# A third PSUM bank in the rotation of two projections, and an earlier load of the first recurrence tile, in a one-layer hybrid backbone

## The chip, the cores and the metric

The kernel runs on one core of a Trainium2 chip. The metric is the device time of one execution in microseconds (us); lower is better. Times of before and after are medians of several runs. One execution was also taken by the hardware profiler; the rows below come from that one.

## What is computed

One layer: a token mixer with three parallel branches, then an expert-choice mixture of experts, for 1024 latent tokens of width 1024 and a prefix of 256 context tokens that only feeds initial states. Cut to what matters here:

```python
proj = h @ p['w_in']                       # h: 1280 x 1024 (context + latents), w_in: 1024 x 7200
u_s5, z, xbc, dt_raw, x_lru, g_lru, gates = split(proj)
ya = s5_branch(u_s5)                       # grouped complex scan, two directions
yb = rmsnorm((ssd_scan(conv(xbc), dt) + D * x) * silu(z)) @ m2_w_out     # Mamba-2, chunks of 128
yc = (rglru_scan(conv(x_lru)) * gelu(g_lru)) @ lru_w_out                 # diagonal recurrence, two directions
g = sigmoid(gates).reshape(.., 3, 1024)
merged = (g[0]*ya + g[1]*yb + g[2]*yc) @ w_o
# then: residual, norm, router, top-k per expert, 16 SwiGLU experts, residual, final norm
```

All large matrix products are made of three passes over operands split into a high and a low part (fp32r), summed in PSUM.

## The kernel before

The program runs through stages whose instructions overlap at the seams. First the modulation and norm of the inputs, which leaves `h` transposed in SBUF as high and low parts (`hxh`, `hxl`). Stage one (pool `p1`) makes the projections `u`, `xbc`, `x_lru` (`xl`) and `g_lru` (`gl`), and the S5 branch, eight groups `hb` one after another (`s5_tab`, `s5_dat`). Stage two (pool `p2`) does the Mamba-2 scan and the RG-LRU recurrence: `states()` carries the chunk states over nine steps, then 32 calls `chunk(g, c)` make the outputs; the four recurrence tiles `lru_tile(t)` are a generator of which the loop takes a step at a time; the projections `z` (8 tasks) and the gates (24 tasks) run in between and fill TensorE. Stage three merges the branches, stage four makes the output product and the routing, stage five the experts.

A projection task loads 128 columns of `w_in` (`load_w`, L117 to L127), splits them on ScalarE and VectorE, and calls `proj_chunk` (L267) for each piece of 512 tokens: 24 matmuls into one PSUM bank (`mm3`, L263 to L265) and an evacuation by ScalarE: `gt` (gelu, L626) for `gl`, `zt` (tanh, L770, with a VectorE step L771 that reads the bank too) for `z`, `gz` (tanh, L778) for the gates. The bank comes from `pbank` (L86), a rotation over two of the eight banks. Five banks belong to a second rotation, `bank`; the last bank has the tag `pm` and is used, in the stretch in question, only by `cx` of `s5_dat` (L526), the context part of the S5 scan.

`lru_tile(t)` begins with a load of the rows `xcd[t]` into `lxc` (L850), a clearing of `lw` on GpSimd (L852), four small loads of weights into `lw` (L855), and casts of both on ScalarE (L858, L863). For t = 0 the program text puts this behind `chunk(0, 0)`.

The order of instructions within each engine is not the text's: outside of the stages whose order is written by hand (stage four on TensorE, stage five), a planner simulates the program when it is built and puts every engine's instructions, SyncE's DMA issues among them, in the order in which its own clock finds them ready; text order is the priority, and evacuations and weight loads are lifted by `high_priority(offset=WPRI)`. On the chip each engine then goes through its queue strictly in that order. A tile of a rotating buffer can be written only when the readers of the tile before it in text order are done.

Of the kernel before, what the change touches and what calls it, by code (L numbers as in the profile page):

```python
# [8 lines left out]
F32 = mybir.dt.float32  # L9
# [9 lines left out]
P = 128  # L19
# [38 lines left out]
def dap(t, off, dims):  # L58
    return bass.AP(tensor=t.tensor, offset=t.offset + off, ap=[list(d) for d in dims])
# [3 lines left out]
def backbone(ctx: ExitStack, tc: tile.TileContext, I, out, dbg=None, stop=None):  # L63
    nc = tc.nc
    V, A, G, T, Y = nc.vector, nc.scalar, nc.gpsimd, nc.tensor, nc.sync
# [14 lines left out]
    psp = psstack.enter_context(tc.tile_pool(name="psp", bufs=1, space=PSUM, reuse_waits="tile"))  # L80
    bankh = [lambda nm: psp.tile([P, 512], F32, tag="b", name=nm, bufs=5)]

    def bank(name):
        return bankh[0](name)

    def pbank(name):  # L86
        return psp.tile([P, 512], F32, tag="pp", name=name, bufs=2)
# [64 lines left out]
    with tc.high_priority(offset=20000):  # L152
        with tc.tile_pool(name="p0", bufs=1, reuse_waits="tile") as p0:
# [26 lines left out]
            pm = bank("pm")  # L180
# [80 lines left out]
    def mm3(ps, wh, wl, xh, xl, nk, first=True, last=True):  # L261
        for k in range(nk):
            T.matmul(ps, wh(k), xh(k), start=(first and k == 0), stop=False)  # L263
            T.matmul(ps, wh(k), xl(k), start=False, stop=False)  # L264
            T.matmul(ps, wl(k), xh(k), start=False, stop=(last and k == nk - 1))  # L265

    def proj_chunk(w, m, nm, evac, c):  # L267
        t0, n, xh, xl, s0 = ((0, 512, hxh, hxl, 0), (512, 512, hxh, hxl, 512), (1024, 256, hch, hcl, 0))[c]
        ps = pbank(f"pj_{nm}_{t0}")
        mm3(ps[:m, :n], lambda k: w[0][:, k, :], lambda k: w[1][:, k, :], lambda k: xh[k][:, s0:s0 + n], lambda k: xl[k][:, s0:s0 + n], KC)  # L270
        with tc.high_priority(offset=WPRI):
            evac(ps, t0, n)
# [7 lines left out]
    xcd = [dr.tile([P, 1283], F32, name=f"xcd{t}") for t in range(4)]  # L280
# [6 lines left out]
    with tc.tile_pool(name="p1", bufs=1, reuse_waits="tile") as p1:  # L287
# [65 lines left out]
        if True:  # L353
# [15 lines left out]
            lr, li = lam[:, 0], lam[:, 1]  # L369
# [311 lines left out]
    with tc.tile_pool(name="p2", bufs=1, reuse_waits="tile") as p2:  # L681
# [7 lines left out]
        la = p2.tile(n3, F32, name="la")  # L689
# [49 lines left out]
        def states():  # L739
            Sp = None  # L740
            v16 = lambda t: t.rearrange("p (h e) -> p h e", h=16)
            for k in range(9):
                st = [bank(f"st{k}_{q}") for q in range(2)]
                for d, c in ((0, cf(k)), (1, cb(k))):
                    xk = p2.tile([P, 1283], F32, tag="xk", name=f"xk{k}{d}", bufs=3)
                    Y.dma_start(xk[:, 0:D].rearrange("p (g e) -> p g e", g=4), xed[c][:, :, 0:256])
                    Y.dma_start(xk[:, D:D + 256], btd[c])
                    xd = p2.tile([P, D], F32, tag="xd", name=f"xd{k}{d}", bufs=2)
                    G.tensor_mul(v16(xd), v16(xk[:, 0:D]), dtd[:, c, d, :, None].to_broadcast([P, 16, 64]))
                    for g in range(4):  # L750
                        T.matmul(st[g // 2][64 * d:64 * d + 64, (g % 2) * 256:(g % 2 + 1) * 256],
                                 xk[:, D + 64 * g:D + 64 * g + 64], xd[:, 256 * g:256 * g + 256], start=True, stop=True)
                Sn = p2.tile([P, D], F32, tag="Sn", name=f"Sn{k}", bufs=2)
                if k > 0:
                    V.tensor_mul(v16(Sn), v16(Sp), decS[:, k, :, None].to_broadcast([P, 16, 64]))
                for q in range(2):
                    sl = slice(q * 512, (q + 1) * 512)
                    if k == 0:
                        V.tensor_copy(Sn[:, sl], st[q])
                    else:  # L760
                        V.tensor_add(Sn[:, sl], Sn[:, sl], st[q])
                if k > 0:
                    Y.dma_start(xed[cf(k + 1)][0:64, :, 256:512], Sn[0:64].rearrange("p (g e) -> p g e", g=4))
                    Y.dma_start(xed[cb(k + 1)][64:128, :, 256:512], Sn[64:128].rearrange("p (g e) -> p g e", g=4))
                Sp = Sn
# [18 lines left out]
        def chunk(g, c):  # L784
# [30 lines left out]
            if c % 4 == 3:  # L815
# [13 lines left out]
                        G.tensor_add(ssum[:, cs], ssum[:, cs], zq[:, t])  # L829
                Y.dma_start(m2_dram[g][:, :, cs], xq)  # L830

        states()
        z_task(0)
        z_task(1)
# [10 lines left out]
        SQE = math.sqrt(EPS)  # L845

        def lru_tile(t):
            lt = lambda nm: p2.tile([P, 1283], F32, tag="xk" if nm in ("lr", "li", "la") else nm, name=f"{nm}{t}", bufs=3 if nm in ("lr", "li", "la") else 1)
            xc = lt("lxc")
            Y.dma_start(xc, xcd[t])  # L850
            lw = p2.tile([P, 2, 2, P], F32, tag="lw", name=f"lw{t}", bufs=1)
            G.memset(lw, 0.0)  # L852
            for e, nm in enumerate(("lru_w_a", "lru_w_x")):
                for hh in range(2):
                    Y.dma_start(lw[64 * hh:64 * hh + 64, e, :, 64 * hh:64 * hh + 64],  # L855
                                dap(I[nm], (2 * t + hh) * 4096, [[64, 64], [8 * 4096, 2], [1, 64]]))
            lwh, lwl = (p2.tile([P, 2, 2, P], F32R, tag=g, name=f"{g}{t}", bufs=1) for g in ("lwh", "lwl"))
            A.copy(lwh, lw)  # L858
            G.tensor_sub(lwl, lw, lwh.bitcast(F32))
            xh_, xl_ = (p2.tile([P, S], F32R, tag="Sn", name=f"lx{g}{t}", bufs=2) for g in "hl")  # L860
            xe_ = p2.tile([P, 2, SC], F32R, tag="lxe", name=f"lxe{t}", bufs=1)
            for o, n, h_, l_ in ((0, S, xh_, xl_), (1027, SC, xe_[:, 0], xe_[:, 1])):
                A.copy(h_, xc[:, o:o + n])  # L863
                G.tensor_sub(l_, xc[:, o:o + n], h_.bitcast(F32))
            yield
            hs = None
            for d in range(2):
                dt_ = 4 * d + t
                col = lambda q: lsc[:, q, dt_:dt_ + 1]
                r, ig = lt("lr"), lt("li")  # L870
                G.memset(r[:, 1024:1027], 0.0)
                G.memset(ig[:, 1024:1027], 0.0)
                for e, dst in enumerate((r, ig)):
                    for (t0, n, h_, l_) in ((0, 512, xh_[:, 0:512], xl_[:, 0:512]), (512, 512, xh_[:, 512:S], xl_[:, 512:S]), (1027, SC, xe_[:, 0], xe_[:, 1])):
                        ps = bank(f"lps{t}{d}{e}{t0}")
                        for q, (w_, x_) in enumerate(((lwh, h_), (lwh, l_), (lwl, h_))):
                            T.matmul(ps[:, :n], w_[:, e, d, :], x_, start=(q == 0), stop=(q == 2))
                        A.activation(dst[:, t0:t0 + n], ps[:, :n], AF.Tanh, bias=lbh[:, e, dt_:dt_ + 1], scale=0.5)
                    yield
                a, q = lt("la"), lt("lq")  # L880
                A.activation(a, r, AF.Exp, scale=col(0), bias=col(0))
                A.activation(q, r, AF.Exp, scale=col(2), bias=col(2))
                A.activation(r, r, AF.Tanh, scale=col(1), bias=col(1))
                V.scalar_tensor_tensor(q, q, 1.0, r, op0=ALU.add, op1=ALU.mult)
                A.activation(q, q, AF.Sqrt)
                V.scalar_tensor_tensor(ig, ig, 1.0, xc, op0=ALU.add, op1=ALU.mult)
                V.scalar_tensor_tensor(ig, q, SQE, ig, op0=ALU.max, op1=ALU.mult)
                if d == 0:
                    V.tensor_tensor_scan(q[:, 1027:1283], a[:, 1027:1283], ig[:, 1027:1283], 0.0, op0=ALU.mult, op1=ALU.add)
                    hs = p2.tile([P, S], F32, tag="xd", name=f"lh{t}", bufs=2)  # L890
                    V.tensor_tensor_scan(hs, a[:, 0:S], ig[:, 0:S], q[:, 1282:1283], op0=ALU.mult, op1=ALU.add)
                else:
                    V.tensor_tensor_scan(q[:, 1027:1283][:, ::-1], a[:, 1027:1283][:, ::-1], ig[:, 1027:1283][:, ::-1], 0.0, op0=ALU.mult, op1=ALU.add)
                    V.tensor_tensor_scan(q[:, 0:S][:, ::-1], a[:, 0:S][:, ::-1], ig[:, 0:S][:, ::-1], q[:, 1027:1028], op0=ALU.mult, op1=ALU.add)
                    V.tensor_add(hs, hs, q[:, 0:S])
                    gl = a[:, 0:S]
                    Y.dma_start(gl, gld[t])
                    V.scalar_tensor_tensor(hs, hs, 0.5, gl, op0=ALU.mult, op1=ALU.mult)
                    Y.dma_start(lru_dram[t], hs)
                yield  # L900
# [46 lines left out]
    with tc.tile_pool(name="p3b", bufs=1, reuse_waits="tile") as p3b:  # L947
# [112 lines left out]
        for d in range(KC):  # L1060
# [5 lines left out]
            for h in range(2):  # L1066
                sl = slice(h * 512, (h + 1) * 512)
                ps = bank(f"bom{d}{h}")
# [42 lines left out]
    li = [dt[0:16, q * P:(q + 1) * P] for q in range(2)]  # L1111
# [230 lines left out]
    with tc.tile_pool(name="p5", bufs=1, reuse_waits="tile") as p5:  # L1342
# [107 lines left out]
        with tc.manual_schedule(engines={mybir.EngineType.DVE, mybir.EngineType.Activation, mybir.EngineType.PE}):  # L1450
# [6 lines left out]
            for s_, (nm, e, j) in enumerate(slots):  # L1457
# [6 lines left out]
                if j == 0:  # L1464
                    tag = {"w1": "h1", "w3": "h3", "w2": "py" if e < 15 else "h1"}[nm]
                    ps = [psp5.tile([P, 512], F32, tag=tag, name=f"{tag}_{nm}{e}{n}", bufs=2) for n in range(2)]
# [125 lines left out]
```

## Time and profile before

| | |
|---|---|
| median of 3 runs | 2032.36 us (2030.41 to 2035.47) |
| profiled execution | 2033.83 us, span of its instructions 2032.0 us |
| TensorE busy | 1878.6 us (92% of the span) |
| VectorE busy | 1583.6 us (78%) |
| ScalarE busy | 1019.4 us (50%) |
| GpSimd busy | 501.1 us (25%) |
| mean granted TensorE clock | 0.965 of full speed |

Rows of an engine's timeline read: start in us, duration in us, engine, line, operation, output<-inputs, shapes, count; in brackets the idle time of that engine just before, and what released it. PE is TensorE, DVE VectorE, ACT ScalarE, POOL GpSimd, SPq the queue of SyncE that issues DMAs. A granted clock of 1.00 is 2.4 GHz, of 0.50 is 1.2 GHz.

### The profile page before, as it was taken

The numbers are of one execution on the slowest core, as the hardware profiler recorded it, in microseconds if no ns is written. First come the engines' busy times: TensorE is split into PE (matmuls) and PEld (weight loads), VectorE is DVE, ScalarE is ACT, GpSimd is POOL, SyncE is SP. The second block draws the span as 40 slices with busy tenths as digits, with TensorE's granted clock in tenths as the row PEclk, the third lists the DMA queues.
The fourth block names the chain that finished last, engine by engine and source line by source line (L and its number), as shares of the span: only waits on it lengthen the run. The fifth ranks groups of instructions, "written<-read, shape, count | busy, mean of one in ns | idle before, by whom it ended". The sixth has DMA issues, their size and how long they took to land.

```text
span 2032.0 us, 26879 instructions
## 1 busy us (share of the span) xinstructions
PE 1878.6 (92%) x9514; PEld 1507.1 (74%) x9514; DVE 1583.6 (78%) x2183; ACT 1019.4 (50%) x1313; POOL 501.1 (25%) x456
## 2 busy tenths in 40 slices
PE   6989999998899999999999999995599999999997
PEld 3678788886666777777777778784488888888885
DVE  4796778876364778887447965599799999999998
ACT  4434444432321765667322122322488887878885
POOL 1463333330053244342000000236201101010142
PEclk8999999998999999999999999998799999999999
DMA  9234334422477676666568863655699999999974
GB/s 326 40 90 116 107 101 117 126 85 69 152 249 215 194 226 187 203 210 198 176 207 298 281 207 125 239 191 201 225 350 405 389 401 393 394 399 394 371 285 166
DMA packets 273127, 462.64 MB, mean 228 GB/s; under 512 B 39968, under 2 KB 167632, under 8 KB 271968
## 3 DMA queue, kind: packets, MB, share of 16 engines
q1 hardware_dynamic: 268672, 445.19, 62.9%
q0 software_dynamic: 4320, 15.73, 3.0%
q8 instruction: 75, 1.23, 0.2%
q14 instruction: 60, 0.49, 0.1%
HBM read 384.44 MB, written 78.51 MB: 228 GB/s over the span
## 4 chain that ended last, share of the span: by engine, by line
PE 36%; DVE 7%; DMA 5%; issue 1%; POOL 1%; SPq 1%; ACT 0%; DVEq 0%; POOLq 0%; ACTq 0%
PE h_w L1472 6%; PE h_w L1473 6%; PE h_w L1474 6%; DMA wm<-in_w_mod_dram 3%; PE py_w L1472 3%; PE py_w L1474 3%; PE py_w L1473 3%; PE wo L1289 2%; PE bom L264 1%; PE bom L263 1%; PE bom L265 1%; DVE tu L1124 1%; PE tb_x L1383 1%; DVE tv L1121 1%; PE tb_h L1383 1%
## 5 line engine op out<-in xcount | busy, mean ns | idle before, releaser
L1367 DVE TENSOR_TENSOR el_w<-er_w,eh_w 128x1024 fp32r<-128x1024 f32 x384 | 459.9, 1220 | 24.7 <-ACT eh_w L1366 11.9
L1366 ACT CAST eh_w<-er_w 128x1024 fp32r<-128x1024 f32 x384 | 403.7, 1052 | 105.7 <-PE h_w L1473 64.7
L1472 PE MATMUL h_w<-eh_w,thi_x 128*128 128x512 f32 x512 | 203.3, 397 | 0.0
L1473 PE MATMUL h_w<-eh_w,tlo_x 128*128 128x512 f32 x512 | 200.5, 392 | 0.0
L1474 PE MATMUL h_w<-el_w,thi_x 128*128 128x512 f32 x512 | 200.2, 391 | 0.0
L263 PE MATMUL pj_gt<-hxh,whi_gt 128*128 128x512 f32 x384 | 153.7, 400 | 8.5 <-ACT gz L778 8.5
L264 PE MATMUL pj_gt<-hxl,whi_gt 128*128 128x512 f32 x384 | 152.9, 398 | 0.0
L265 PE MATMUL pj_gt<-hxh,wlo_gt 128*128 128x512 f32 x384 | 152.2, 396 | 0.0
L1474 PEld LDWEIGHTS h_w<-el_w,thi_x 128*128 128x128 f32 x512 | 96.5, 189 | 20.8 <-DVE el_w L1367 0.2
L1473 PEld LDWEIGHTS h_w<-eh_w,tlo_x 128*128 128x128 f32 x512 | 96.6, 189 | 19.5 <-DVE tlo_x L1391 0.4
L1472 PEld LDWEIGHTS h_w<-eh_w,thi_x 128*128 128x128 f32 x512 | 96.6, 189 | 19.5 <-ACT thi_x L1390 0.2
L1375 POOL DMA_INDIRECT xs<-h2d,idx x16 | 24.0, 1498 | 293.9 <-PE tb_x L1383 273.4
L1472 PE MATMUL py_w<-eh_w,thi_h 128*128 128x512 f32 x240 | 96.4, 402 | 0.0
L1473 PE MATMUL py_w<-eh_w,tlo_h 128*128 128x512 f32 x240 | 93.9, 391 | 0.0
L1474 PE MATMUL py_w<-el_w,thi_h 128*128 128x512 f32 x240 | 93.9, 391 | 0.0
L263 PEld LDWEIGHTS pj_gt<-hxh,whi_gt 128*128 128x128 f32 x384 | 73.3, 191 | 27.3 <-ACT gz L778 10.8
L804 POOL TENSOR_TENSOR dec<-dec,bc 128x512 f32<-128x512 f32 x32 | 64.8, 2024 | 93.2 <-ACT dec L795 86.0
L1408 POOL DMA_INDIRECT accd<-ysm,idx x14 | 49.8, 3560 | 149.3 <-DVE ysm L1406 138.9
L265 PEld LDWEIGHTS pj_gt<-hxh,wlo_gt 128*128 128x128 f32 x384 | 73.2, 191 | 15.9 <-issue 0.2
L264 PEld LDWEIGHTS pj_gt<-hxl,whi_gt 128*128 128x128 f32 x384 | 73.2, 191 | 15.9 <-issue 0.3
L1197 POOL TENSOR_TENSOR r_wo<-r_wo,bc_m 128x1024 f32<-128x1024 f32 x4 | 10.2, 2540 | 279.1 <-DMA mgm<-mgd 138.8
L799 DVE TENSOR_TENSOR rowb<-rowb,XL 128x1024 f32<-128x1024 f32 x32 | 49.9, 1560 | 36.9 <-ACT dec L795 36.9
(649 smaller groups left out, 5046.5 us busy)
## 6 DMA issues: line engine op xcount, KB each, us to landing
er_w<-in_moe_w_dram SPq DMA_DIRECT2D x384, 512.0 KB
rowb<-rowsd SPq DMA_DIRECT2D x32, 512.0 KB
wm<-in_w_mod_dram SPq DMA_DIRECT2D x32, 512.0 KB
raw_gt<-in_w_in_dram SPq DMA_DIRECT2D x24, 512.0 KB
gtd<-gz SPq DMA_DIRECT2D x48, 256.0 KB
xk<-xed SPq DMA_DIRECT2D x18, 512.0 KB
wm<-in_w_mod_dram SPq DMA_DIRECT2D x8, 1024.0 KB
xe<-xed SPq DMA_DIRECT2D x32, 256.0 KB
```

The lines of the kernel that those rows point to most:

```text
L263: T.matmul(ps, wh(k), xh(k), start=(first and k == 0), stop=False)
L264: T.matmul(ps, wh(k), xl(k), start=False, stop=False)
L265: T.matmul(ps, wl(k), xh(k), start=False, stop=(last and k == nk - 1))
L799: V.tensor_sub(rowb, rowb, XL[:, c, :, 4 * g:4 * g + 4][:, :, :, None].to_broadcast(sh))
L804: G.tensor_mul(dec, dec, Cd[:, None, :].to_broadcast([P, 4, P]))
L1289: T.matmul(st4[i]["ps"][n], ms[i][a][:, k], wo[k][b][:, sl], start=(k == 0 and q == 0), stop=(k == KC - 1 and q == 2))
L1366: A.copy(a, raw)
L1367: V.tensor_sub(b, raw, a.bitcast(F32))
L1408: G.indirect_dma_start(out=accd[:, :], out_offset=bass.IndirectOffsetOnAxis(ap=idx[:, e:e + 1], axis=0), in_=yss[e], in_offset=None, compu ...
L1472: T.matmul(ps[n], xa[:, j, :], a[:, sl], start=(j == 0), stop=False)
L1473: T.matmul(ps[n], xb[:, j, :], a[:, sl], start=False, stop=False)
L1474: T.matmul(ps[n], xa[:, j, :], b[:, sl], start=False, stop=(j == KC - 1))
```

## The change

`proj_chunk` counts its calls; each third call takes its bank from the tag `pm` where the task's name begins with z or g, which are `z`, the gates (`gt`) and `gl`. The first part of `lru_tile(t)` (the load of `lxc`, the clearing of `lw`, its four loads) becomes a function `lru_in(t)`; for t = 0 it is called in front of `states()`, for the other tiles where it stood.

```diff
+    pn = [0]
+
     def proj_chunk(w, m, nm, evac, c):
         t0, n, xh, xl, s0 = ((0, 512, hxh, hxl, 0), (512, 512, hxh, hxl, 512), (1024, 256, hch, hcl, 0))[c]
-        ps = pbank(f"pj_{nm}_{t0}")
+        pn[0] += 1
+        ps = psp.tile([P, 512], F32, tag="pm", name=f"pj_{nm}_{t0}", bufs=1) if pn[0] % 3 == 2 and nm[0] in "zg" else pbank(f"pj_{nm}_{t0}")
...
+        lt_ = lambda nm, t: p2.tile([P, 1283], F32, tag="xk" if nm in ("lr", "li", "la") else nm, name=f"{nm}{t}", bufs=3 if nm in ("lr", "li", "la") else 1)
+
+        def lru_in(t):
+            xc = lt_("lxc", t)
+            Y.dma_start(xc, xcd[t])
+            lw = p2.tile([P, 2, 2, P], F32, tag="lw", name=f"lw{t}", bufs=1)
+            G.memset(lw, 0.0)
+            for e, nm in enumerate(("lru_w_a", "lru_w_x")):
+                for hh in range(2):
+                    Y.dma_start(lw[64 * hh:64 * hh + 64, e, :, 64 * hh:64 * hh + 64],
+                                dap(I[nm], (2 * t + hh) * 4096, [[64, 64], [8 * 4096, 2], [1, 64]]))
+            return xc, lw
+
+        lin0 = [lru_in(0)]
         states()
...
         def lru_tile(t):
-            lt = lambda nm: ...
-            xc = lt("lxc")
-            Y.dma_start(xc, xcd[t])
...
+            lt = lambda nm: lt_(nm, t)
+            xc, lw = lin0.pop() if lin0 else lru_in(t)
```

## Rows read from the trace of the kernel before

**Rows 1.** Busy time of stage two and of one stall: stretch, length, engines, granted clock, DMA, GB/s.

```profile
560.00:700.00 140.00, 140.00 (x654) 100.47 (x654) 83.96 (x81) 43.46 (x57) 54.30 (x30) 1.00 0.69 213
700.00:985.00 285.00, 263.79 (x1414) 205.25 (x1413) 232.51 (x194) 183.40 (x236) 102.60 (x63) 0.96 0.64 204
985.00:1043.00 58.00, 55.54 (x246) 45.21 (x246) 18.18 (x17) 22.83 (x22) 1.66 (x1) 1.00 0.53 165
...
720.00:735.00 15.00, 11.69 (x52) 9.26 (x51) 14.97 (x11) 5.00 (x7) 9.60 (x6) 0.78 0.64 210
```

**Rows 2.** Who TensorE waited for, 463 to 560: us in total, times, longest.

```profile
PE pj_z L263 <- DVE zt L771: 6.3, 1, 6.3
PE yp L575 <- DVE ea L568: 5.2, 2, 3.6
PE yp L576 <- DVE eb L571: 3.4, 2, 2.0
PE pj_gl L263 <- ACT gt L626: 2.4, 2, 1.2
```

**Rows 3.** Timeline of all engines around the stall of `z`, at 550.

```profile
549.97 0.40 ACT L863 CAST lxe<-lxc 128x256 fp32r<-128x256 f32 x1 [11.94 <-DMA lxc<-xcd]
...
551.52 0.59 ACT L770 ACTIVATE zt<-pj_z 128x512 f32<-128x512 f32 x1
...
552.15 0.69 DVE L771 SCALAR_TENSOR_TENSOR zt<-zt,pj_z 128x512 f32<-128x512 f32 x1 [12.56 <-ACT zt L770]
...
552.89 0.80 PE L263 MATMUL pj_z<-hxh,whi_z 128*128 128x512 f32 x1 [6.35 <-DVE zt L771]
```

**Rows 4.** SyncE's queue ahead of it: issues of the states' and the tile's loads.

```profile
529.28 6.08 SPq L746 DMA_DIRECT2D xk<-xed  x1
...
542.78 0.32 SPq L850 DMA_DIRECT2D lxc<-xcd  x1
543.20 2.14 SPq L855 DMA_DIRECT2D lw<-in_lru_w_a_dram  x2
```

**Rows 5.** GpSimd's timeline: the states' first multiplication.

```profile
560.60 1.91 POOL L749 TENSOR_TENSOR xd<-xk,dtd 128x1024 f32<-128x1024 f32 x1 [7.05 <-PE prw L726]
```

**Rows 6.** Busy time around the stalls, columns as in Rows 1.

```profile
473.00:478.00 5.00, 4.63 (x20) 4.34 (x20) 2.36 (x10) 0.24 (x1) 0.00 (x0) 0.50 0.01 2
478.00:483.00 5.00, 4.10 (x10) 3.30 (x11) 2.02 (x3) 1.33 (x3) 0.00 (x0) 0.53 0.51 184
507.00:512.00 5.00, 3.82 (x21) 3.63 (x21) 0.00 (x0) 1.17 (x3) 0.53 (x1) 0.70 0.38 105
512.00:523.00 11.00, 11.00 (x49) 9.11 (x50) 0.00 (x0) 1.00 (x2) 0.00 (x0) 1.00 0.35 121
...
553.00:558.00 5.00, 5.00 (x12) 3.92 (x13) 4.36 (x19) 3.86 (x8) 0.53 (x1) 0.52 0.69 216
```

**Rows 7.** TensorE's timeline, 463 to 480: `cx`, the waits of `yp` and of `gl`.

```profile
463.33 1.87 PE L529 MATMUL cx<-U,Pm 128*128 128x32 f32 x16
...
478.90 0.80 PE L263 MATMUL pj_gl<-hxh,whi_gl 128*128 128x512 f32 x1 [1.18 <-ACT gt L626]
```

**Rows 8.** ScalarE's and VectorE's timelines there: evacuations of `gl`, and a weight split.

```profile
478.25 1.08 ACT L626 ACTIVATE gt<-pj_gl 128x512 f32<-128x512 f32 x2
...
492.77 1.23 DVE L126 TENSOR_TENSOR wlo_gl<-raw_gl,whi_gl 128x1024 fp32r<-128x1024 f32 x1 [10.22 <-ACT whi_gl L125]
```

**Rows 9.** Who TensorE waited for, 560 to 1045, the three largest.

```profile
PE pj_gt L263 <- ACT gz L778: 8.5, 6, 3.2
PE yps L813 <- DVE rowb L803: 7.5, 3, 3.6
PE yps L813 <- ACT gz L778: 4.5, 2, 3.3
```

**Rows 10.** VectorE's timeline at the seam to stage three.

```profile
1031.24 1.23 DVE L978 TENSOR_TENSOR ylo_l<-yr_l,yhi_l 128x1024 fp32r<-128x1024 f32 x1 [2.39 <-ACT yhi_l L977]
1042.79 1.76 DVE L958 TENSOR_TENSOR wlo_f<-raw_s,whi_s 128x1536 fp32r<-128x1536 f32 x1 [10.32 <-PE pj_gt L264]
```

More of the change, by code (lines that the diff above doesn't have):

```diff
@@ L847, in lru_tile @@
         def lru_tile(t):
-            lt = lambda nm: p2.tile([P, 1283], F32, tag="xk" if nm in ("lr", "li", "la") else nm, name=f"{nm}{t}", bufs=3 if nm in ("lr", "li", "la") else 1)
-            xc = lt("lxc")
-            Y.dma_start(xc, xcd[t])
[L851 to L856, printed above, removed]
+            lt = lambda nm: lt_(nm, t)
+            xc, lw = lin0.pop() if lin0 else lru_in(t)
             lwh, lwl = (p2.tile([P, 2, 2, P], F32R, tag=g, name=f"{g}{t}", bufs=1) for g in ("lwh", "lwl"))
```

## The prediction

> **What bounds the kernel now.** I read the page's totals first, then the busy time of stage two by stretch, then the waits of TensorE, and last the timelines around each wait. TensorE is busy for 92% of the span, so the question is only where it idles and whether the change reaches those places. Both edits act between the end of stage one (from 463 us) and the last gate (1043 us). In [rows 1] the reader is to see that from 560 to 700 TensorE does not pause at all, that from 700 to 985 it lacks 285.0 - 263.8 = 21.2 us, and that up to 1043 it lacks 2.5 us. In all of that time projections wait to be made, so a microsecond of TensorE that is not idled away is a microsecond off the end of the stage, as long as nothing else is later there. [Rows 10] say how far that holds: the last operand that stage three needs, `ylo_l`, is done at 1031.24 + 1.23 = 1032.5, and the first weights of that stage wait 10.32 us for the last gate. So the loop's tail has some 10 us of room for the gates to end earlier by themselves; where the whole loop moves forward, its tail moves along and more passes through. What follows (merge, output product, experts) starts from there and is moved as a whole.
>
> **The stall of z, and the load that causes it.** [Rows 3] are one chain, read from the bottom: TensorE stands for 6.35 us at a piece of `z` until VectorE's `zt` frees the bank; `zt` waits for ScalarE's `zt`; ScalarE has that in its queue behind the cast `lxe<-lxc`, for which it stood for 11.94 us, until the rows of the recurrence tile landed. Nobody needs that cast soon; it only stands first in a queue that is kept in order. [Rows 4] show why it is late: the load is issued at 542.78, behind the states' loads, and lands at 549.97, 7.2 us later.
>
> The change takes it in front of the states' loads. What it moves there: one clearing on GpSimd, the load of `lxc` (0.32 us of SyncE's time) and four loads of `lw`, two pairs of at most 2.14 us, 4.6 us of SyncE's queue in all [rows 4]. Nine steps of `states` with their loads are passed by it and so come up to 4.6 us later. Cover: the first multiplication of the states waits at 560.60 for something that comes through TensorE (`prw`), not for its rows [rows 5], and TensorE has `z` to do meanwhile. If that cover went, the 4.6 us would fall into the stretch that is busy for 140 of 140 us [rows 1], where they cost nothing until `z` runs out.
>
> Does the load then come in time? ScalarE asked for it at 549.97 - 11.94 = 538.0. In the worst case it inherits the slow issue of 6.08 us in [rows 4], goes out at 535.4 and lands 7.2 us later, at 542.6: `zt` on ScalarE would then start some 1.5 us later (as it did after 549.97), at 544.2, and VectorE's part, 0.6 us after that start and 0.7 us long, would be done at 545.5, before TensorE asks at 552.89 - 6.35 = 546.5. So the 6.35 us go, by this edit alone. Next late there is nothing up to 700 that the rows show.
>
> The third bank reaches the same stall by itself: of three banks in turn, the piece that stalled gets the one that was freed a piece earlier. So these two edits share this term and it is counted once.
>
> The clock comes on top. After the stall twelve matmuls take 5.00 us at a granted clock of 0.52, about the lower level of 1.2 GHz; in an undisturbed stretch 49 take 11.00 us, 0.224 us each, at 1.00 (2.4 GHz) [rows 6]. What the slow stretch loses is its busy time times the missing clock: 5.00 x 0.48 = 2.4 us. **Term one: 6.35 + 2.4 = 8.7 us**, bounds 0 (another instruction of ScalarE's queue takes the cast's place) and 8.7.
>
> **The end of stage one.** `gl` begins with g and takes part in the rotation. [Rows 2] list what TensorE waits for between 463 and 560: 5.2 + 3.4 us for the S5 scan's results (`yp`), 2.4 us for evacuations of `gl`, 11.0 in all beside `z`. Twice the same thing happens: both banks hold finished pieces of `gl`, their evacuation stands behind S5's own output on ScalarE (478.25, [rows 8]), and TensorE has nothing to do while VectorE scans. The first time costs 3.6 + (3.4 - 2.0) + 1.2 = 6.2 us of waiting and, by [rows 6], 4.63 x 0.50 + 4.10 x 0.47 = 4.2 us of clock; the second time 1.6 + 2.0 + 1.2 = 4.8 and 3.82 x 0.30 = 1.1. A third bank lets one more piece run in there: 24 matmuls, 24 x 0.224 = 5.4 us, about as long as the hole. A second effect goes the same way: VectorE idles 10.22 us for a weight split whose buffer the late `gl` holds [rows 8], and the S5 chain of the last group stands behind it.
>
> The added wait: the bank `pm` is also that of `cx`, the S5 context product. The second piece of the first `gl` task now sits between two `cx`, so the last `cx` (16 matmuls, at 463.33, [rows 7]) must wait for that piece's evacuation; at the old place in ScalarE's queue that ends at 478.25 + 1.08 = 479.3. Behind the last `cx` on TensorE is whatever the planner puts there; on VectorE its sums come just ahead of a part that idled for 10.22 us. So it is cheap if `cx` is put behind `yp`, and costs a wait of up to 479.3 - 463.3 = 16 us if something needed stands behind it. Bounds of the term: 11.0 + 5.3 = 16.3 us gained, and, for the added wait less what is gained, nothing gained. **Term two: 7.0 us**, two thirds of the first hole's 10.4, as the row nearest to it is one piece of 5.4 us and a part of the clock; the second hole is left as it is.
>
> One rule speaks against this. The Trainium skill, page "TensorE: Matmul & The Clock Gate", section "HAM oscillation — how this bites in real kernels", reports of a measured kernel that adding double-buffering of PSUM gave no further gain. By it the sum would hold term one alone. The trace agrees only where TensorE is fed without a break, in the 140 us of [rows 1]; in [rows 2, 9] it waits for evacuations by name.
>
> **The gates.** In the loop, waits whose last releaser is the gates' evacuation come to 8.5 us at the gates themselves and 4.5 at `yps` behind them, eight in all, the longest 3.2 and 3.3 [rows 9]. A third bank covers 5.4 us, more than any of them. But the planner knows of the third bank as well, and will run gates further ahead, until it is full again; and the long stalls stand where VectorE is busy for 14.97 of 15 us [rows 1], so that the hole would only reopen at `yps`. Bounds: 13.0 us and the clock of two long stalls (11.69 x 0.22 = 2.6 each) gained, 18.2; or as much lost as the third rival says. **Term three: 2.0 us**, a third of the short ones (8.5 + 4.5 - 3.2 - 3.3 = 6.5).
>
> **Sum.** 8.7 + 7.0 + 2.0 = 17.7 us off the profiled execution's 2033.83: **2016.1 us**. That execution lies 1.5 us above the median of the three runs and within their spread of 5 us; I do not correct for it.
>
> **Rivals.** *Only the load counts.* The planner fills the third bank at once and TensorE waits as before, for three pieces instead of two: 2033.8 - 8.7 = 2025.1. For it: the two edits overlap in term one, and VectorE is full at the long stalls. Against it: the holes of stage one, with evacuations queued behind S5's output.
>
> *It cancels out.* The planner's new order is another order for 580 us, and its clock is not the chip's: the stall of `z` itself is a load that it must have believed to be early. A long stall in the loop costs 3.3 + 2.6 = 5.9 us; three new ones are 17.7 and eat the sum: 2033.8, between 2028 and 2038. Against it: [rows 3] name a queue order that the edit removes, whatever the rest.
>
> *Slower: gates ahead of the scan.* Place: the loop of 32 chunks. With three banks one more gate piece of 5.4 us stands ahead of `yps` on TensorE, and its evacuation, lifted in priority, ahead of the exponentials of `dec` and `rowb` on ScalarE; VectorE, the fullest engine there, waits, and `yps` with it. The 7.5 us of waits for `rowb`, three times, are of this kind [rows 9]. Each new one costs 5.9; from three on nothing is left, five make 29.5 - 17.7 = 11.8 us more: 2045.6. Against it: VectorE works 232.5 of 285 us in the loop, so it has room on average.
>
> **How the numbers follow.** My forecast 0.53, only the load 0.20, cancelled 0.15, slower 0.12. A measurement of this kernel tells about 0.3%, 6 us, from no change, that is 2026 to 2038. So faster 0.73 (the first two), same 0.15, slower 0.12. The range goes from 2000 (both holes of stage one closed, 16.3, and half of the gates' 18.2, beside term one: 2033.8 - 34.1) to 2033, which takes in the load alone and about half of the cases that cancel. The first case's own range is 2000 to 2024.
>
> **What would show it.** Right: no wait of ScalarE for `lxc` near 540, `zt` without a wait of VectorE over 5 us, the states' first multiplication about 10 us earlier against the first `z`; fewer than 6 us of waits for `yp` and `gl`; no stretch at half clock after the first `z`. Wrong: `lxc` still issued after the states' loads; `cx` standing in TensorE's queue for `gl`'s evacuation; more than three waits over 3 us of `yps` in the loop; or stage three beginning no earlier than 1035 because `ylo_l` is late.

## The result, and the profile after

The changed kernel takes 2011.09 us (median; 2008.87 to 2013.96) against 2031.38 us for the kernel before on the same chip: ratio 0.9896, 95% interval 0.9881 to 0.9910. The forecast was 2016.1 us, a ratio of 0.991 to its profiled execution. The direction and the size are right; the reason given for half of it is not, and that is what the experiments are about.

TensorE's busy time is 5.6 us lower than before (1878.6), which is the same work with less of it at the slow clock; the other 14.2 us of the span's difference are idle time that went:

```profile
PE 1873.0 (93%) x9514; PEld 1503.9 (75%) x9514; DVE 1586.2 (79%) x2183; ACT 1020.2 (51%) x1313; POOL 497.3 (25%) x456
```

To see where, I cut both traces at three marks that both kernels have: the last matmul of each of the projections `gl`, `z` and gates (starts of the last L265 of each). From first to last `gl`: 71.4 us before, 58.2 after. To the last `z`: 136.6 and 135.4. To the last gate: 383.2 and 378.4. From there to the end: 989.4 and 987.8. The first `gl` comes 1.0 us later. 13.2 + 1.2 + 4.8 + 1.6 - 1.0 = 19.8 us, the difference of the two spans (2032.0 and 2012.2). So the end of stage one gave more than forecast, the stretch of `z` gave almost nothing, and the gates gave more than forecast.

The busy time by stretch, columns as in [rows 1]:

```profile
473.00:478.00 5.00, 3.16 (x24) 2.78 (x24) 1.26 (x4) 1.90 (x4) 0.00 (x0) 1.00 0.24 71
478.00:483.00 5.00, 5.00 (x23) 4.12 (x23) 1.77 (x3) 0.71 (x2) 0.00 (x0) 1.00 0.69 243
507.00:512.00 5.00, 5.00 (x24) 4.13 (x23) 0.04 (x1) 1.12 (x2) 0.00 (x0) 1.00 0.47 160
...
520.00:525.00 5.00, 5.00 (x24) 4.14 (x23) 2.57 (x6) 0.00 (x0) 0.00 (x0) 1.00 0.07 9
...
530.00:540.00 10.00, 5.14 (x15) 3.35 (x14) 7.21 (x26) 6.19 (x10) 2.44 (x3) 0.75 0.99 311
540.00:550.00 10.00, 10.00 (x46) 8.13 (x45) 6.38 (x14) 3.35 (x8) 3.77 (x2) 0.91 0.65 188
...
700.00:985.00 285.00, 266.93 (x1415) 209.58 (x1414) 224.60 (x193) 175.66 (x227) 100.46 (x61) 0.96 0.63 199
```

At the end of stage one the granted clock is 1.00 throughout, where [rows 6] had 0.50, 0.53 and 0.70. From 530 on a new hole stands: TensorE is busy for 5.14 of 10 us, at a mean granted clock of 0.75. Who TensorE waited for, 463 to 560, answers to [rows 2]:

```profile
PE pA L697 <- DVE la L693: 4.9, 1, 4.9
PE pj_gl L263 <- ACT gt L629: 2.4, 2, 1.2
PE yp L579 <- DVE eb L574: 0.7, 1, 0.7
PE yp L578 <- DVE ea L571: 0.3, 1, 0.3
```

The two waits of `yp`, 5.2 + 3.4 us, are down to 1.0. The wait of `z` for its bank, 6.35 us, is gone, and a wait of 4.9 us stands at the first matmul of the states (`pA`). The chain behind it, all engines in order of time, answers to [rows 3, 4]:

```profile
514.36 1.34 SPq L736 DMA_DIRECT2D Dc<-in_m_d_dram  x2
515.76 0.61 SPq L839 DMA_DIRECT2D lxc<-xcd  x1
516.47 7.14 SPq L844 DMA_DIRECT2D lw<-in_lru_w_a_dram  x2
...
517.52 0.58 ACT L773 ACTIVATE zt<-pj_z 128x512 f32<-128x512 f32 x1
529.78 0.41 ACT L873 CAST lxe<-lxc 128x256 fp32r<-128x256 f32 x1 [11.68 <-DMA lxc<-xcd]
...
531.24 1.04 ACT L125 CAST whi_z<-raw_z 128x1024 fp32r<-128x1024 f32 x1
...
532.31 1.45 DVE L126 TENSOR_TENSOR wlo_z<-raw_z,whi_z 128x1024 fp32r<-128x1024 f32 x1 [9.57 <-ACT whi_z L125]
...
535.96 0.49 DVE L693 SCALAR_TENSOR_TENSOR la<-dt,arow 128x320 f32<-128x320 f32 x1
...
536.51 1.43 PE L697 MATMUL pA<-la,mle 128*128 128x320 f32 x2 [4.86 <-DVE la L693]
```

Read from the bottom it is the chain of [rows 3] with another last link. ScalarE stands for the rows of the recurrence tile as long as before, 11.68 us instead of 11.94. The load is indeed issued early, at 515.76, ahead of the states' loads; but it lands 14.0 us later, not 7.2, and SyncE is held right behind it (7.14 us for two issues that took 2.14 in [rows 4]). VectorE idles 9.57 us for a weight split, the softplus of `dt` and `la` are queued behind that, and TensorE runs dry.

At the gates, 560 to 1045, the first three, against [rows 9]:

```profile
PE yps L816 <- issue: 15.4, 7, 4.0
PE yps L816 <- ACT rowb L804: 1.3, 1, 1.3
PE pcb L800 <- ACT lr L888: 1.0, 1, 1.0
```

The waits of the gates themselves (8.5 us) and of `yps` for their evacuation (4.5) are gone; what is left stands at `yps`, 15.4 us for which the trace names no releaser.

### The profile page after: what moved, and what is told of

Read it like the earlier page. It is cut to its first block, busy times and chain, and to the rows that moved or that the text cites. A ratio compares the mean times of both kernels' runs of the same rounds, so it can differ in the third digit from the quotient of the medians.

```text
span 2012.2 us, 26882 instructions
## 1 busy us (share of the span) xinstructions
PE 1873.0 (93%) x9514; PEld 1503.9 (75%) x9514; DVE 1586.2 (79%) x2183; ACT 1020.2 (51%) x1313; POOL 497.3 (25%) x456
## 2 busy tenths in 40 slices
DMA packets 273127, 462.64 MB, mean 230 GB/s; under 512 B 39968, under 2 KB 167632, under 8 KB 271968
## 4 chain that ended last, share of the span: by engine, by line
PE 57%; DVE 8%; DMA 5%; issue 3%; ACT 2%; SPq 1%; POOL 1%; DVEq 0%; ACTq 0%; POOLq 0%
PE h_w L1482 6%; PE h_w L1483 6%; PE h_w L1484 6%; PE pj_gt L263 3%; PE pj_gt L265 3%; PE pj_gt L264 3%; PE py_w L1482 3%; PE py_w L1484 3%; PE py_w L1483 3%; PE wo L1299 2%; PE st L754 2%; DMA wm<-in_w_mod_dram 2%; PE bom L264 1%; PE bom L263 1%; PE bom L265 1%
## 5 line engine op out<-in xcount | busy, mean ns | idle before, releaser
L265 PE MATMUL pj_gt<-hxh,wlo_gt 128*128 128x512 f32 x384 | 153.3, 399 | 0.0
L265 PEld LDWEIGHTS pj_gt<-hxh,wlo_gt 128*128 128x128 f32 x384 | 73.3, 191 | 16.8 <-issue 0.8
L265 PE MATMUL pj_xb<-hxh,wlo_xb 128*128 128x512 f32 x192 | 76.8, 400 | 0.5 <-DVE wlo_xb L126 0.5
```

## The experiments

All medians below are of the kernel beside runs of the kernel before on the same chip; the ratio is to those. Stretches are those of the section above, in us; the last column is the largest wait of TensorE between the last `gl` and the early states. Stretches are differences of starts read to a tenth, from one profiled execution each. These lie up to 6 us from their kernels' medians (load first: 2004.53 us against 2010.67), so a difference of one or two microseconds in one stretch is not read as an effect. With the third bank the gates take 375.3 to 379.7 us over all kernels, without it 381.5 to 383.2.

| kernel | median, ratio [95%] | gl | z | gates | TensorE's wait in z's stretch |
|---|---|---|---|---|---|
| before | 2031.38 to 2034.4 | 71.4 | 136.6 | 383.2 | z for zt 6.3 |
| whole change | 2011.09, 0.9896 [0.9881, 0.9910] | 58.2 | 135.4 | 378.4 | pA for la 4.9 |
| load only | 2034.22, 1.0004 [0.9995, 1.0014] | 71.0 | 137.4 | 383.2 | z for zt 7.8 |
| bank only | 2011.32, 0.9896 [0.9881, 0.9911] | 58.2 | 135.8 | 377.5 | prw for XA 5.9 |
| bank, gl only | 2022.0, 0.9934 [0.9920, 0.9947] | 58.2 | 136.8 | 382.9 | z for zt 5.7 |
| bank, z and gates only | 2029.19, 0.9974 [0.9963, 0.9985] | 71.3 | 136.3 | 378.2 | prw for XA 6.3 |
| Dc behind the states | 2009.82, 0.9883 [0.9868, 0.9898] | 58.3 | 135.7 | 377.4 | st for xd 5.3 |
| load first | 2010.67, 0.9893 [0.9876, 0.9911] | 58.2 | 133.1 | 379.7 | st for xd 3.6 |
| whole change, Dc in rows | 2003.04, 0.9852 [0.9838, 0.9866] | 58.2 | 127.8 | 376.5 | none |
| softplus early | 2013.46, 0.9902 [0.9888, 0.9916] | 59.5 | 144.0 | 375.3 | st for xd 9.1 |
| bank, Dc in rows | 2003.83, 0.9853 [0.9838, 0.9868] | 58.2 | 127.7 | 379.2 | none |
| before, Dc in rows | 2023.81, 0.9954 [0.9941, 0.9968] | 71.1 | 127.8 | 381.5 | none |
| load only, Dc in rows | 2023.77, 0.9955 [0.9942, 0.9969] | 71.0 | 128.1 | 382.0 | none |
| load first, Dc in rows | 2002.21, 0.9842 [0.9829, 0.9856] | 58.3 | 127.7 | 378.5 | none |

**The two edits apart.** The load alone is the kernel before with

```diff
+        lin0 = [lru_in(0)]          # lxc, lw of tile 0, ahead of states()
...
-            xc = lt("lxc")
-            Y.dma_start(xc, xcd[t])
...
+            xc, lw = lin0.pop() if lin0 else lru_in(t)
```

> Only the early load, two banks. Theory A (the prediction's term one: the early load by itself ends the 6.35 us stall of z and its clock): 8.7 us under before, about 2023. Theory B (from the trace after: ScalarE's wait for lxc has only moved, 11.94 us at 549.97 to 11.68 us at 529.78, because the planner puts the cast lxe forward together with the load, and SyncE's queue holds the load back by the 7.14 us issue behind Dc): no gain. ScalarE then waits some 11 us one piece of z earlier, the second z piece's evacuation comes late, and TensorE stalls 5 to 8 us at the fourth piece; time within 5 us of before, 2027 to 2036.

The bank alone is the other half:

```diff
+    pn = [0]
...
-        ps = pbank(f"pj_{nm}_{t0}")
+        pn[0] += 1
+        ps = psp.tile([P, 512], F32, tag="pm", ...) if pn[0] % 3 == 2 and nm[0] in "zg" else pbank(...)
```

> Only the third bank, the load where it was. Theory A: the stall of z is closed by the bank just as well, the end of stage one gains as in the changed kernel: about the same as the changed kernel, 2009 to 2013. Theory B: ScalarE still waits about 11 us for lxc, but at a place where three banks cover it, and the chain of dt to pA is already done by then, so the 4.9 us wait of pA for la in the changed kernel is not there either: 4 to 8 us faster than the changed kernel, 2003 to 2007.

Measured: 1.0004 for the load, as Theory B had it, and 0.9896 for the bank, 2011.32 us, where Theory A had 2009 to 2013; Theory B's 2003 to 2007 was missed. The early load gives nothing and the bank gives all. Two rows of the load-only kernel's timeline show why the prediction's first term did not come:

```profile
538.70 0.41 ACT L870 CAST lxe<-lxc 128x256 fp32r<-128x256 f32 x1 [11.92 <-DMA lw<-in_lru_w_x_dram]
...
543.70 0.79 PE L263 MATMUL pj_z<-hxh,whi_z 128*128 128x512 f32 x1 [7.80 <-DVE zt L771]
```

The stall of `z` is still there, and longer. In the bank-only kernel `z` no longer stalls, but the next instructions that need VectorE's and ScalarE's held results do:

```profile
540.70 1.89 PE L729 MATMUL prw<-ident,XA 128*32 128x128 f32 x8 [5.91 <-DVE XA L704]
```

**The bank by its users.** The third bank for `gl` alone (`nm[:2] == "gl"` in place of `nm[0] in "zg"`), without the load:

> The third bank for gl alone, the load where it was. Theory C (from the traces so far: of the 20 us, the end of stage one gives 13.2, since gl takes 58.2 us from its first to its last matmul instead of 71.4; the z phase gives about 1, the gates about 5): 13 us under before, 2017 to 2021. Theory A (the prediction's sizes: 7 at the end of stage one, 8.7 at the stall of z): 2022 to 2027.

And for `z` and the gates alone:

> The third bank for z and the gates, not for gl, the load where it was. Theory C: the end of stage one stays at 71 us, the z phase gains 1 to 2, the gates about 5: 5 to 8 us under before, 2024 to 2028. Theory A: the stall of z goes (8.7) and the gates give 2: 2020 to 2023. Rival (the gates gain only because they start earlier and meet the loop differently): within 3 us of before.

Measured: 0.9934 and 0.9974, which by the ratio is 13.4 and 5.3 us under the kernel before on that chip: the gains of Theory C. Its ranges in absolute time were missed (2022.00 against 2017 to 2021, 2029.19 against 2024 to 2028), where the kernel before took 2034.40 us, more than on the other chips; 2022.00 lies at the edge of Theory A's range, and it is the stretches that decide for C. The two shares, 0.66% and 0.26%, add up to 0.92%, against 1.04% for both. `gl`'s stretch is 58.2 us with the first and 71.3 with the second; the gates' is 382.9 and 378.2. So the 13.2 us and the 4.8 us are two separate effects of the same edit, each in the stretch of the projection that uses the bank. Without the bank on `gl` the waits of [rows 2] stand unchanged, as the waits of the kernel with `z` and gates only show:

```profile
PE prw L729 <- DVE XA L704: 6.3, 1, 6.3
PE yp L578 <- DVE ea L571: 5.2, 2, 3.6
PE yp L579 <- DVE eb L574: 3.4, 2, 2.0
```

**What holds the load.** In every trace so far the queue of SyncE is held for 6.1 to 6.5 us at the third issue behind the two loads of `Dc`, whichever load that is: `xk` in [rows 4] (6.08), the second of the two `lw` issues after the change. Each load of `Dc` is only 2 KB, but its access pattern (64 rows of eight elements with a stride of two) takes them in 512 pieces of 4 bytes. In that time hardly any bytes move: 9 GB/s at a DMA share of 0.07 in the stretch 520 to 525 above. What does move is small pieces: from 517 to 524 the trace after the change has 760 DMA packets, all under 512 bytes and 0.00 MB in sum, about 109 per us. At that pace the 1024 pieces of the two loads take about 9.4 us, an estimate from this row; so the queue stands while `Dc` itself is being fetched. Four kernels were made to test what holds the queue. First, the whole change with `Dc` loaded behind `states()`:

```diff
-        Dc = p2.tile([P, 8], F32, name="Dc")          # ahead of lru_in(0) and states()
-        for hh in range(2):
-            Y.dma_start(Dc[64 * hh:64 * hh + 64, :], dap(I["m2_d"], hh, [[0, 64], [2, 8]]))
...
+        # the same three lines behind states()
```

> The changed kernel with the two loads of Dc (64 x 8 pieces of 4 bytes each) moved from in front of the recurrence tile's load to behind the states. Theory B1 (those two loads hold SyncE's queue and the transfers behind them for 6 to 7 us: the long issue of 6.08 before and 7.14 after is the third one behind them): lxc, issued at about 514, lands by 522 instead of 529.8, ScalarE waits 0 to 4 us instead of 11.7, the 4.9 us wait of pA for la and its half clock (about 2.4 us) go: 2002 to 2006. Rival B2 (the long issue belongs to the moment or to lxc and lw themselves, whose rows are short): lxc still lands 14 us after its issue and the time stays within 3 us of the changed kernel, 2008 to 2014.

Measured: 0.9883, no clear gain over 0.9896. `lxc`, now ahead of `Dc`, is issued at 513.48 and its cast starts at 519.93 after a wait of 1.41 us, as B1 had it; the time, 2009.82 us, is what B2 had. The hold went with `Dc` and fell on what is now behind it, spread over several issues. The timeline, all engines:

```profile
522.54 1.49 SPq L849 DMA_DIRECT2D Dc<-in_m_d_dram  x2
524.07 3.90 SPq L789 DMA_DIRECT2D bc<-bcd  x3
...
530.35 2.61 SPq L122 DMA_DIRECT2D raw_z<-in_w_in_dram  x1
533.06 4.32 SPq L841 DMA_DIRECT2D lw<-in_lru_w_a_dram  x1
...
556.76 1.27 ACT L795 ACTIVATE dec<-rowb 64x512 f32<-64x512 f32 x2 [13.50 <-DMA rowb<-rowsd]
558.11 2.33 POOL L804 TENSOR_TENSOR dec<-dec,bc 128x512 f32<-128x512 f32 x1 [10.91 <-ACT dec L795]
...
565.55 3.67 PE L751 MATMUL st<-xd,xk 128*64 128x256 f32 x8 [5.33 <-POOL xd L749]
```

GpSimd stands 10.91 us for ScalarE's `dec`, which waits for a DMA of `rowb`; `xd` is behind it in GpSimd's queue, and TensorE waits 5.33 us for `xd`, at the fourth group of eight of the states' matmuls. That `rowb` comes late because of the hold is read from these rows and not shown by a run of its own.

Second, the whole change with `lru_in(0)` at the very head of stage two, before softplus, `arow` and `Dc`:

```diff
+        lin0 = [lru_in(0)]          # first lines of stage two
...
-        lin0 = [lru_in(0)]          # behind Dc
```

> The changed kernel with the call that loads the first recurrence tile put at the very start of stage two, ahead of the loads of arow and Dc. B1: lxc goes out ahead of Dc, lands within 7 us of its issue at about 513.7, by 521; lw too goes out ahead of Dc. ScalarE's wait for lxc falls to 0 to 3 us, pA's wait for la goes: 2002 to 2007. B2: the long issue stays with lw or lxc, time within 3 us of the changed kernel.

Measured: 0.9893, 2010.67 us, above B1's 2002 to 2007. The wait for `lxc` falls to 1.99 us, the hold is back on the states' loads, and TensorE waits 3.6 us at the fourth group of the states' matmuls:

```profile
517.28 5.25 SPq L763 DMA_DIRECT2D xk<-xed  x1
...
561.14 3.36 PE L768 MATMUL st<-xd,xk 128*64 128x256 f32 x8 [3.63 <-POOL xd L766]
```

Third, on top of that, the softplus of `dt` made in stage one already (at `hb == 6`, in tiles of that stage) and `Dc` behind the states:

```diff
+            if hb == 6:
+                softplus(dt, 320, p1, "d", early=True)
...
-        softplus(dt, 320, p2, "d")
```

> The changed kernel with the tile's load first in stage two, Dc's loads behind the states, and the softplus of dt (13 small VectorE and 2 ScalarE instructions, all inputs there since the start) made during stage one, under the S5 groups. Theory D (the stall of 4 to 6 us that each variant shows at another instruction near the first states is one chain, softplus, la, pA, XA, prw, rows to DRAM and back, that TensorE's planned order does not leave room for): the chain ends 10 us or more earlier, the stall and its slow stretch go, 5 to 9 us under the changed kernel, 2002 to 2006. Rival (the planner orders by a clock without the transfers' real time, and will put the next waiting instruction in front): another wait of 4 to 6 us, time 2007 to 2013.

Measured: 0.9902. Theory D's 2002 to 2006 was missed. Taking the softplus out of VectorE's part ahead of the states was no cure: the fourth group of the states' matmuls now waits 9.1 us for `xd`, and the hold shows as one issue of 7.89 us (`szd`) behind `Dc`. As `Dc` and the load moved too, this kernel does not price the softplus alone; the next one shows that the softplus can stay where it was.

Fourth, the whole change with the same numbers fetched in 128 rows of 64 bytes and taken apart by VectorE:

```diff
+        D16 = p2.tile([P, 16], F32, name="D16")
+        Y.dma_start(D16, dap(I["m2_d"], 0, [[0, P], [1, 16]]))
...
-            Y.dma_start(Dc[64 * hh:64 * hh + 64, :], dap(I["m2_d"], hh, [[0, 64], [2, 8]]))
+            V.tensor_copy(Dc[64 * hh:64 * hh + 64, :], D16[64 * hh:64 * hh + 64, hh::2])
```

> The changed kernel with Dc loaded as one row of 16 values to every partition (128 pieces of 64 bytes) and taken apart by two copies on VectorE, instead of 2 x 512 pieces of 4 bytes. If the 4-byte pieces are what holds SyncE's queue for 6 to 7 us: no issue over 2 us in the ten behind Dc, lxc lands within 7 us of its issue instead of 14, ScalarE's wait for it falls from 11.7 us to under 4. If the place in the program does it: the long issue stays. The time, by what moving Dc gave (a new wait a little later takes the gain): within 4 us of the changed kernel, 2007 to 2013, under both.

Measured: 0.9852, 0.44% under the whole change. What was expected of the 4-byte pieces came: no long issue behind `Dc`, and a wait of 2.90 us for `lxc`; the time, expected within 4 us of the whole change, was missed. No issue behind it is held, and TensorE has no wait left between the last `gl` and the states: `z`'s stretch is 127.8 us instead of 135.4.

**The rows with and without the rest.** This left open whether the early load is needed once the queue is free. The same edit of `Dc` was put on the bank alone, on the kernel before, on the load alone, and on the kernel with the load first.

> The third bank, the weights and rows of tile 0 loaded behind the states as before, and Dc loaded as 128 rows of 64 bytes. The bank alone measured 0.9896 of before, the whole change with these Dc rows 0.9852. Theory H (the long hold of SyncE's queue behind Dc's four-byte pieces is the whole second obstacle; with it gone, where the load of lxc stands matters little): 0.984 to 0.987, the stretch from the last gl matmul to the last z matmul 128 us, as in the whole change with the rows. Rival J (the early load and the clean queue are both needed: each takes away a wait behind which the same 6 us appear again): 0.988 to 0.991, that stretch 133 to 136 us, and a stall of 4 us or more of TensorE before the first states.

> The kernel before with Dc loaded as 128 rows of 64 bytes, nothing else. Theory H: 0.995 to 0.997 of before (6 to 9 us less), z's stretch about 129 us instead of 136.6, no issue of SyncE over 4 us behind Dc. Rival J: 0.999 to 1.001, z's stretch 135 us or more; SyncE's long issue is gone, but ScalarE still waits for lxc or VectorE's XA comes late, and TensorE stalls 4 us or more.

> The early load without the third bank, and Dc loaded as 128 rows of 64 bytes. The early load alone measured 1.0004. Both theories: 0.995 to 0.997 of before, z's stretch 128 to 130 us, ScalarE's wait for lxc under 4 us instead of 11.7, no stall of z. It tells whether the prediction's first term (8.7 us for the early load) holds where the queue isn't held: read beside the kernel with the Dc rows alone, Theory H has the two equal, Rival J has this one 6 us or more faster. If z's stretch stays at 136 us, both are wrong and the bank is needed for the gain of the Dc rows.

> The whole change, the first recurrence tile's loads put at the head of stage two (ahead of softplus and arow), and Dc loaded as 128 rows of 64 bytes. The whole change with the Dc rows measured 0.9852; there TensorE has no wait left in z's stretch. Both theories: within 0.002 of that (0.983 to 0.987), z's stretch 127 to 129 us: the wait of ScalarE for lxc that is left (2.9 us) goes, but nothing on TensorE waits for it any more. If another 2 us or more are gained, ScalarE's queue still set the pace.

Measured: 0.9853, 0.9954, 0.9955 and 0.9842. Theory H holds in all four; Rival J, by which the load is needed too, is refuted by the first and by the pair in the middle. With rows the early load is worth 0.9955 against 0.9954, and 0.9852 against 0.9853: nothing, as without them. The rows alone are worth 0.46%, 9 us, whether the bank is there or not (0.9896 x 0.9954 = 0.9851, measured 0.9853). In the kernel before with nothing changed but `Dc`, the timeline of SyncE and ScalarE reads, against [rows 3, 4]:

```profile
525.37 0.38 SPq L733 DMA_DIRECT2D D<-in_m_d_dram  x1
525.80 0.58 SPq L748 DMA_DIRECT2D xk<-xed  x1
526.43 0.61 SPq L749 DMA_DIRECT2D xk<-btd  x1
527.15 0.57 SPq L748 DMA_DIRECT2D xk<-xed  x1
...
531.65 0.60 SPq L852 DMA_DIRECT2D lxc<-xcd  x1
...
533.66 0.59 ACT L772 ACTIVATE zt<-pj_z 128x512 f32<-128x512 f32 x1
539.04 0.41 ACT L865 CAST lxe<-lxc 128x256 fp32r<-128x256 f32 x1 [4.79 <-DMA lw<-in_lru_w_x_dram]
```

The issue that took 6.08 us takes 0.57, and `lxc` goes out 6.3 us behind the load of `D` instead of 16.3 behind `Dc`, from its old place in the program text. ScalarE still waits, 4.79 us (the row names the last of several transfers), but TensorE no longer notices. The busy time there, columns as in [rows 1]:

```profile
530.00:535.00 5.00, 5.00 (x24) 4.13 (x22) 3.41 (x9) 1.55 (x2) 0.00 (x0) 1.00 1.03 346
...
533.00:543.00 10.00, 10.00 (x46) 8.22 (x45) 8.62 (x18) 3.79 (x8) 2.06 (x3) 1.00 0.96 295
543.00:553.00 10.00, 10.00 (x49) 7.99 (x47) 8.82 (x29) 5.69 (x11) 2.26 (x2) 1.00 0.60 181
```

The DMA engines move 346 GB/s where the change's stretch behind `Dc` had 9, and TensorE is busy without a break at full clock. The fastest kernel is the whole change with the load first and `Dc` in rows, 0.9842; the bank with the rows alone, 0.9853, cannot be told from it, and both beat the change as it was made (0.9896).

## Why the prediction was right, and where it was not

**The sum.** 17.7 us were forecast and 20.3 measured between the medians, by other shares than forecast: 8.7, 7.0 and 2.0 were said for the stall of `z`, the end of stage one and the gates; the stretches show 1.2, 13.2 and 4.8. That the sum came so close is luck: one term fell away and the two others were each about twice as large. Of the signs that the prediction named itself, the waits for `yp` and `gl` did fall under 6 us, to 3.4. ScalarE's wait for `lxc` did not go, it ended at 529.78 instead of 549.97, and a slow clock still followed the first `z` (0.75 from 530 to 540).

**Term one failed, at "Does the load then come in time?".** The price was right: with the hold gone, `z`'s stretch is 8.8 us shorter (136.6 to 127.8), against 6.35 + 2.4 = 8.7. What failed is that the early load would earn it, "by this edit alone". Two things were taken as fixed that moved with the edit. One is the landing: 7.2 us after the issue in [rows 4], but the issue at 515.76 lay behind `Dc` and took 14.0. The other is the time at which ScalarE asks, put at 538.0: the planner moved the cast forward with its load, behind the first `zt` instead of the second, from 11.5 us after `Dc`'s issue (538.0 - 526.5, its issue in the trace of before) to 3.7 (529.78 - 11.68 - 514.36). The rows came 8.0 us earlier by the same measure (549.97 - 526.50 = 23.5; 529.78 - 514.36 = 15.4). Load and asker moved by the same 8 us, so the wait stayed at 11.7. The bound of 0 for this term had the mechanism nearly in words, another instruction of ScalarE's queue in the cast's place; it was the same cast in an earlier place. That the third bank reaches the same stall by itself was half right: `z` did not stall, but ScalarE stood for `lxc` about as long (11.43 us with the bank alone), and the wait came out at `prw` or `pA` instead (5.9, 4.9 us).

The row that would have told was in the working: an issue of 6.08 us beside issues of 0.32 to 1.1 in [rows 4], read as a worst case and not asked for its cause. The Trainium skill says, page "Perfetto Trace Analysis", section "DMA Instruction — HWDGE (DVE, Sync)", that the profiled time of such an issue covers the wait for the descriptor generator and the generating, not the movement of the data. The trace agrees in so far as the two issues of `Dc` took 1.34 us together and small packets went on for microseconds behind them. That the long issue behind them waited for `Dc`'s pieces only the runs show. At which place of the DMA path it is held no run here shows, and that stays open.

**Term two was under-sized.** 7.0 us were taken of at most 16.3, and 13.2 came (13.4 us by the ratio of the kernel with the bank on `gl` alone). The step that went wrong is "the second hole is left as it is": both holes closed, but for 3.4 us. Of 11.0 us of waits those 3.4 are left, which gives 7.6, and the 5.3 us of slow clock are gone entirely; 12.9 in all. The first hole gave 8.3 of it (4.1 of waits, 4.2 of clock), where 7.0 were forecast, and the second 4.6 (3.5 and 1.1), where nothing was. The second effect, named but not priced, went too: VectorE's 10.22 us of idling for the late weight split, with the last group's S5 chain behind it. How much each of the two gave no run separates. The rows of the kernel after, around the first hole, answer to [rows 7, 8]:

```profile
477.14 1.57 ACT L629 ACTIVATE gt<-pj_gl 128x512 f32<-128x512 f32 x3
...
477.78 0.50 PE L263 MATMUL pj_gl<-hxh,whi_gl 128*128 128x512 f32 x1 [1.18 <-ACT gt L629]
...
483.36 1.87 PE L532 MATMUL cx<-U,Pm 128*128 128x32 f32 x16
484.40 1.22 DVE L126 TENSOR_TENSOR wlo_gl<-raw_gl,whi_gl 128x1024 fp32r<-128x1024 f32 x1 [1.10 <-ACT whi_gl L125]
...
486.15 0.28 DVE L536 TENSOR_TENSOR ta<-cx,co 128x128 f32<-128x128 f32 x1
```

Three pieces of `gl` are evacuated together instead of two, and the split comes at 484.40 instead of 492.77, with 1.10 us of waiting. The added wait went as the prediction had it in its cheap case: `cx` now runs at 483.36, behind `yp`, and VectorE asks for its result only at 486.15, when it has been done for 0.9 us; nobody waits for it.

The rule of the Trainium skill that was weighed, page "TensorE: Matmul & The Clock Gate", section "HAM oscillation — how this bites in real kernels", reports for one measured kernel no further gain from double-buffering of PSUM. Going from two banks to three measured 0.9934 on `gl` alone here, so that report does not carry over to this kernel; in [rows 2] TensorE waits for an evacuation by name and for the S5 results that stand in the same stretch.

**Term three was under-sized.** 2.0 us forecast, 4.8 measured (5.0 in the kernel with the bank on `z` and gates only). The gates' own waits went from 8.5 us to nothing. `yps` waited 13.9 us before (7.5 and 4.5 in [rows 9], and smaller ones of 1.2 and 0.7) and 17.1 after (15.4, 1.3, 0.2 and 0.2), so 3.2 us came back there, and 8.5 - 3.2 = 5.3 remain. That a hole would reopen at `yps` was right; that it would take back nearly all was not.

**The rivals.** That only the load counts is refuted by both halves: the load gave 1.0004, the bank everything. That it cancels out is refuted by the ratio of 0.9896. Slower by gates ahead of the scan: `yps` does wait 3.2 us more, mostly in seven waits of at most 4.0 for which the trace names no releaser, so that it is not shown to be by that mechanism; and the gates' own waits gave 8.5 us. The tail held as expected: `ylo_l` was done ahead of the last gate, and stage three's first split still waits for that gate, 5.50 us where it was 10.32 in [rows 10]:

```profile
1024.57 1.76 DVE L968 TENSOR_TENSOR wlo_f<-raw_s,whi_s 128x1536 fp32r<-128x1536 f32 x1 [5.50 <-PE pj_gt L264]
```

## What to carry to other kernels

A stall's price and its cure are two claims: that removing it is worth 8.7 us can be read from the rows, but what removes it must be tried against everything that shares its cause, for a load that is moved forward can take its consumer forward with it where a planner orders the queues, as here, and it inherits whatever holds its own queue. An issue that takes ten times as long as its like is the first row to explain, and what stands a few issues ahead of it is the first suspect. A small gather in 4-byte pieces can be worth fetching as whole rows and taking apart on an engine with room: here that gave another 0.44% beside the change's 1.04%.

## What the runs showed of the hardware

Two loads of 2 KB each, in 512 pieces of 4 bytes, held SyncE's queue for 5 to 8 us at one issue, with two to four issues in between: 6.08 us at `xk` before, 6.07 with the bank only, 5.25 with the load first, 7.89 at `szd` with the softplus early. With `Dc` behind the states the hold was spread over issues of 2.24, 2.61 and 4.32 us. While it lasted in the trace after the change, from 517 to 524, the DMA engines moved about 109 small packets per us and hardly any bytes. The same values as 128 rows of 64 bytes took one issue of 0.38 us and two copies, and held nothing; the execution has 912 packets fewer by its page (272215 instead of 273127), and 9 us of the whole kernel hung on it. Whether the number of the pieces or their size does it no run separates.
